# A hybrid decoder step: TensorE's issue order in the mixing stage, array shapes of its sample steps, and the bank of a transposed page

## The chip, the cores and the metric

The kernel runs on one core of one Trainium2 chip. The metric is the time of one execution on the device, in microseconds (us); the figure for a kernel is the median of several executions. Before the change it is 1176.64 us, the median of 3 runs (1175.74 to 1176.77).

In the profile PE is the matrix engine (TensorE), PEld its weight loads, DVE is VectorE, ACT is ScalarE, POOL is GpSimd, SP issues most DMAs.

## The reference

One layer for 512 new prompt tokens and 8 x 4 sample tokens: a half-step SwiGLU FFN, a token mixer, a second half-step FFN. The change lies in the mixer.

```python
def token_mix(h, past_k, past_v, C0, n0, m0, rel_bias, lam_init,
              w_in, b_gates, lam_q, lam_k, attn_norm, mlstm_norm, w_out):
    proj = h @ w_in
    ...
    q_a, k_a, v_a, q_m, k_m, v_m, o_m, gates = jnp.split(proj, idx, axis=-1)
    ...
        attn = diff_attention(q_a, k_all, v_all, q_pos, k_pos, rel_bias, lam)
    attn = (rmsnorm(attn, attn_norm) * (1.0 - lam_init)).reshape(B, S, H_ATT * ATT_DV)
    ...
    h_m, C, n, m = mlstm_chunkwise(...)
    h_m = rmsnorm(h_m, mlstm_norm).astype(h.dtype).reshape(B, S, H_ML * ML_DH) * jax.nn.sigmoid(o_m)
    mixed = jnp.concatenate([attn.astype(h.dtype), h_m], axis=-1)
    return mixed @ w_out, k_rows, v_a, C, n, m

def diff_attention(q, k, v, q_pos, k_pos, rel_bias, lam):
    logits = jnp.einsum('bqhcd,bkhcd->bchqk', q, k, preferred_element_type=jnp.float32) * (ATT_DQ ** -0.5)
    ...
    p = jax.nn.softmax(logits, axis=-1)
    a = p[:, 0] - lam * p[:, 1]
    return jnp.einsum('bhqk,bkhd->bqhd', a.astype(v.dtype), v)
```

There are 4 attention heads and 4 mLSTM heads of width 128. A sample's past keys and values, 512 rows, lie in pages of 128 rows that a page table picks from a cache.

## The kernel before

Activations are held with features on partitions and the 544 tokens (512 prompt, 32 sample) as columns, in two halves of 288 and 256 tokens. Every weight product is computed to about fp32 precision from two parts of each operand: L222, L223 and L224 multiply high by high, high by low and low by high. One output tile of 128 features and one half of the tokens takes 8 contraction tiles x 3 = 24 matmuls, into one bank of the pool `acc` (three banks). A weight tile is loaded as `raw` (SP), its high part `wh` is cast on ACT (L208), its low part `wl` subtracted on DVE (L209).

The mixing stage is a row of such products (q, k, v of each attention head; q, k, v of each mLSTM head; the output gates; then w_out), and between them run the heads' own steps. Those are written as Python generators in five queues of `side` (`prep`, `attn`, `ml`, `mls`, `smp`); `run` (L1350) advances every queue by one step after each product half. A step ends at a `yield`.

- `attn_head` (L896) starts one `attn_block` per 128 queries, up to three at a time. A block's scores are L958 (four matmuls; 128, 256, 384 or 512 keys wide). Their operands are split as well: `key_parts` (tile `cs`, L930 on ACT and L931 on DVE) once a head, and `query_parts` (tile `vb`, L940 on ACT and L942 on DVE) once a block; `vb` has one buffer, so a block's queries are split after the block before has used its own. The softmax follows on DVE (L966) and ACT (L969), then transposes L984, the value product L990, a norm, and the transpose L892 in `head_out`.
- `attn_samples` (L1000) gathers key pages from the cache (L1007, POOL, tile `pgin`, seven buffers), transposes each with four fp32 matmuls (L1033), copies it out on ACT (L1034, tile `pgT`), and multiplies it with the sample queries: the scores L1021 (page pairs) and L1060 (new keys), then transposes L1079 and L1084 of the probabilities, and the value products L1092 and L1096. L1021, L1060, L1092 and L1096 address 32 columns of the array at a time, four heads or samples beside one another; everything else uses 128. The mLSTM's L1254 is of the 32-column kind too.
- `ml_head` (L1133) runs an mLSTM head in four chunks: per chunk the state update L1170, the numerator L1178 and L1180, `ml_norm` (L1121; ACT and DVE), and L892 of the chunk before. `ml_sample_head` (L1211) updates the sample states.
- `out_gate` (L1298) is the gate product; behind each of its halves the queue `ml` is advanced twice.

PSUM has the pools `acc` (3 banks), `aux` (3, head steps) and `smp` (2, sample steps).

What sets the order: the instructions of each engine stand in a list that the scheduler of the language builds. By default it does not keep the program's order but places instructions by its own estimate of when they are ready, so that a step's matmuls may stand in the middle of a product, or another step's matmuls in the middle of a step. A context `tc.manual_schedule(engines=...)` keeps the named engines in the program's order; before the change only the kernel's setup uses it.

Of the kernel before, what the change touches and what calls it, by code (L numbers as in the profile page):

```python
# [10 lines left out]
F32 = mybir.dt.float32  # L11
# [165 lines left out]
class _Builder:  # L177
# [718 lines left out]
    def attn_head(self, h, k, v, side):  # L896
        nc = self.nc
        hd = self.hd
        kt = hd.tile([128, 4, 128], F32, name="kt")
        vt = hd.tile([128, 4, 132], F32, name="vt")  # L900
        for qb in range(4):
            side.add("attn", self.attn_block(h, qb, self.X[:, 4 + h, :], k, vt))
            if qb < 2:
                yield
        self.tok_major(v, vt[:, :, 0:128])
        nc.gpsimd.dma_start(out=self.o["v_prompt"][0, 0].rearrange("(b p) h d -> p b h d", p=128)[:, :, h, :],
                            in_=vt[:, :, 0:128])
        yield
        self.tok_major(k, kt)
        nc.gpsimd.dma_start(out=self.o["k_prompt"][0, 0].rearrange("(b p) h d -> p b h d", p=128)[:, :, h, :], in_=kt)  # L910
        nc.vector.tensor_copy(out=self.kas[:, h, :], in_=k[:, SEQ:T])
        nc.vector.tensor_copy(out=self.vas[:, h, :], in_=v[:, SEQ:T])
        self.new_keys += 1
# [31 lines left out]
    def attn_block(self, h, qb, q, k, vt):  # L945
        nc = self.nc
        wk = self.wk
        n = (qb + 1) * 128
        if qb == 0:
            self.key_parts(k)  # L950
            self.query_parts(q[:, 0:n])
            yield
        P = []
        z = wk.tile([128, 6], F32, name="z", bufs=6)
        for c in range(2):
            ps = self.ps_tile()
            for a in range(2):
                nc.tensor.matmul(ps[:, 0:n], lhsT=self.qt[:, 2 * a + c, :], rhs=self.ks[c][:, 0:n],  # L958
                                 start=a == 0, stop=a == 1)
            L = wk.tile([128, 512], F32, name="L", bufs=5)  # L960
            f = max(n - 256, 0)
            strip = self.strip[:, h, :]
            if f:
                nc.vector.tensor_tensor_reduce(L[:, 0:f], ps[:, 0:f], strip[:, 0:1].to_broadcast([128, f]), 1.0, -3.0e38,
                                               ALU.add, ALU.max, z[:, 4 + c:5 + c])
            nc.vector.tensor_tensor_reduce(L[:, f:n], ps[:, f:n], strip[:, 256 - n + f:256], 1.0,  # L966
                                           z[:, 4 + c:5 + c] if f else -3.0e38, ALU.add, ALU.max, z[:, c:c + 1])
            nc.vector.tensor_scalar_mul(z[:, c:c + 1], z[:, c:c + 1], -1.0)
            nc.scalar.activation(out=L[:, 0:n], in_=L[:, 0:n], func=AF.Exp, bias=z[:, c:c + 1],  # L969
                                 accum_out=z[:, 2 + c:3 + c])  # L970
            P.append(L)
        self.blocks_left -= 1
        if qb < 3:
            self.query_parts(q[:, n:n + 128])
        nc.vector.reciprocal(out=z[:, 2:4], in_=z[:, 2:4])
        nc.vector.tensor_tensor(out=z[:, 3:4], in0=z[:, 3:4], in1=self.nlam, op=ALU.mult)
        nc.vector.tensor_scalar(out=P[1][:, 0:n], in0=P[1][:, 0:n], scalar1=z[:, 3:4], scalar2=None, op0=ALU.mult)
        nc.vector.scalar_tensor_tensor(out=P[0][:, 0:n], in0=P[0][:, 0:n], scalar=z[:, 2:3], in1=P[1][:, 0:n],
                                       op0=ALU.mult, op1=ALU.add)
        yield  # L980
        yield
        ps = self.ps_tile()
        for kb in range(qb + 1):
            nc.tensor.transpose(ps[:, kb * 128:kb * 128 + 128], P[0][:, kb * 128:kb * 128 + 128], self.ident)  # L984
        aT = wk.tile([128, 512], F32, name="aT", bufs=2)
        nc.scalar.copy(out=aT[:, 0:n], in_=ps[:, 0:n])
        yield
        po = self.ps_tile()
        for kb in range(qb + 1):
            nc.tensor.matmul(po[:, 0:128], lhsT=aT[:, kb * 128:kb * 128 + 128], rhs=vt[:, kb, 0:128],  # L990
                             start=kb == 0, stop=kb == qb)
        y = wk.tile([128, 128], F32, name="y", bufs=3)
        nc.scalar.activation(out=y, in_=po[:, 0:128], func=AF.Square, accum_out=z[:, 4:5])
        self.rstd_act(z[:, 4:5], DH, z[:, 4:5])
        nc.vector.tensor_scalar(out=y, in0=po[:, 0:128], scalar1=z[:, 4:5], scalar2=None, op0=ALU.mult)
        yield
        self.head_out(y, self.X[:, h, qb * 128:qb * 128 + 128], 0)


    def attn_samples(self):  # L1000
# [4 lines left out]
        def page(which, b, pg):  # L1005
            t = self.pg.tile([128, 512], F32, name="pgin", bufs=7)
            nc.gpsimd.indirect_dma_start(out=t[:, 0:512], out_offset=None, in_=caches[which],  # L1007
                                         in_offset=IndirectOffsetOnAxis(ap=self.idx[:, b * NPG + pg:b * NPG + pg + 1], axis=0))
            return t[:, 0:512]
# [5 lines left out]
        for g in range(2):  # L1015
            lg = self.smp.tile([128, 512], F32, name="smp")
            todo_scores = []

            def scores(p, j, kT):
                for h in range(H):  # L1020
                    nc.tensor.matmul(lg[32 * h:32 * h + 32, p * 256:p * 256 + 256], lhsT=self.qz[:, 4 * g + j, h, :],  # L1021
                                     rhs=kT[:, h, :], start=j == 0, stop=j == 3, tile_position=(0, 32 * h))
            for p in range(NPG // 2):
                for j in range(4):
                    kT = self.pg.tile([128, H, 256], F32, name="pgT", bufs=3)
                    for e in range(2):
                        kp = ahead.pop(0)
                        i = todo.index((g, 2 * p + e, j)) + AHEAD
                        if i < len(todo):
                            ahead.append(page(0, 4 * todo[i][0] + todo[i][2], todo[i][1]))  # L1030
                        ps = self.smp.tile([128, 512], F32, name="smp")
                        for h in range(H):
                            nc.tensor.transpose(ps[:, h * 128:h * 128 + 128], kp[:, h * 128:h * 128 + 128], self.ident)  # L1033
                        nc.scalar.copy(out=kT[:, :, e * 128:e * 128 + 128], in_=ps.rearrange("p (h k) -> p h k", h=H))  # L1034
                    if len(todo_scores) == 2:
                        while todo_scores:
                            scores(*todo_scores.pop(0))
                    todo_scores.append((p, j, kT))
                    if p == 1 and j == 1:
                        vps = [page(1, 4 * g + jj, 0) for jj in range(4)]  # L1040
                    yield
            if g == 0:
                while self.new_keys < H:
                    yield
                for src, dst, name in ((self.vas, vtok, "v_sample"), (self.kas, None, "k_sample")):
                    ps = self.smp.tile([128, 512], F32, name="smp")
# [30 lines left out]
            ps = self.smp.tile([128, 512], F32, name="smp")  # L1077
# [35 lines left out]
            ps = self.smp.tile([128, 512], F32, name="smp")  # L1113
# [206 lines left out]
    def mix(self, hs, ws, gpost, finish, before):  # L1320
        nc, tc = self.nc, self.tc
# [15 lines left out]
        with ExitStack() as ctx:  # L1337
# [10 lines left out]
            def tile_of(name):  # L1348
                return self.hd.tile([128, T], F32, name=name)
# [10 lines left out]
            with gkp as gk:  # L1360
# [4 lines left out]
                k, v = tile_of("k"), tile_of("v")  # L1365
# [10 lines left out]
                for half in range(2):  # L1376
                    ps = [self.acc_tile(half)]
# [42 lines left out]

            self.new_keys = 0
            self.blocks_left = 4 * H
            side.add("prep", self.attn_head(0, k, v, side))
            run(project(*((aq[h], asc) for h in range(1 + NQ, H))))
            for h in range(H):
# [6 lines left out]
            for h in range(1, H):  # L1432
                k, v = tile_of("k"), tile_of("v")
# [35 lines left out]
            def mixed(half):  # L1469
                a, b = self.h_tiles(half)  # L1470
                for k in range(KT):
                    y = self.X[:, k, self.cols(half)]
                    nc.scalar.copy(out=a[:, k, :], in_=y)
                    nc.vector.tensor_tensor(out=b[:, k, :], in0=y, in1=a[:, k, :].bitcast(F32), op=ALU.subtract)
                ms.append((a, b, None))
# [9 lines left out]
            def mat(i, m, w, half):  # L1485
                if i == 3:
                    nc.scalar.dma_start(out=self.X[:, :, self.cols(half)], in_=xd[:, :, self.cols(half)])
                ps = self.acc_tile(half)
                _run(self.mmh(ps, w, ms, half))
                self.post_evac(ps, m, half, gpost, i == 0)  # L1490
            mixed(0)
            for i in range(KT):
                mat(i, *ws[max(0, i + KEPT - KT)], 0)
# [148 lines left out]
```

## Time and profile before

| | |
|---|---|
| median of 3 runs | 1176.64 us (1175.74 to 1176.77) |
| the profiled execution | 1174.52 us |
| its span in the profile | 1172.7 us |
| its mean granted TensorE clock | 0.997 |
| products of the mixing section, 456.66 to 735.87: L222, L223, L224 | 126.3, 123.9 and 123.1 us busy |
| L1033, page transposes | 19.5 us busy |
| L958, attention scores | 17.5 us busy, 3.8 us idle before them |
| L1096 and L1021, sample values and scores | 13.3 and 11.0 us busy |

The span is the time from the first to the last recorded instruction; the execution's own time is 1.8 us more. Busy times of matmuls overlap, since a matmul is recorded until it has left the array while the next is already streaming; what one costs is read from the distance of starts. A row of a timeline gives the start, the time, the engine, the line, the operation, output and inputs with their shapes (`128*32` is an operand of 32 array columns), and how many matmuls are joined in the row; in brackets stands how long the engine was idle before it and what ended that.

### The profile page before, as it was taken

Reading aid. Unit: us, or ns where it says so; the run is one execution under the profiler, and the core shown is the slowest. Engines: PE = TensorE matmul, PEld = TensorE weight load, DVE = VectorE, ACT = ScalarE, POOL = GpSimd, SP = SyncE. Lnnn points to the kernel's source line nnn. Section 1 sums busy time; section 2 is a strip of 40 time slices with the busy share of each in tenths; the row PEclk is TensorE's granted clock in tenths of the full one; section 3 lists DMA queues with packets and bytes.
Section 4 is the critical chain, followed back from the end, with each engine's and each line's share of the span. In section 5 each row is a group of like instructions: output and inputs, shape, how many; then the busy total and the mean of one; then the engine's idle time right before and its main releaser. Section 6 shows DMA issues by size and latency. Waiting matters only on the chain.

```text
span 1172.7 us, 22926 instructions
## 1 busy us (share of the span) xinstructions
PE 1154.3 (98%) x9182; PEld 1116.9 (95%) x9182; DVE 654.4 (56%) x1633; ACT 524.6 (45%) x1259; POOL 113.4 (10%) x155
## 2 busy tenths in 40 slices
PE   8999999999999999999999999999999999999997
PEld 7999999999999998899789879999999999999997
DVE  6755454554223698668675567885545454522334
ACT  6533332333323565767554456763333333332333
POOL 0000000000000043421234441000000000000000
PEclk9999999999999999999999999999999999999999
DMA  7322322222333464543355554532322322133334
GB/s 190 127 73 74 106 89 93 73 93 80 99 91 108 134 178 143 172 136 86 91 162 166 181 158 159 170 103 78 108 73 73 108 85 97 50 99 99 100 99 126
DMA packets 157545, 132.89 MB, mean 113 GB/s; under 512 B 5437, under 2 KB 149157, under 8 KB 157440
## 3 DMA queue, kind: packets, MB, share of 16 engines
q1 hardware_dynamic: 146576, 102.00, 29.2%
q0 software_dynamic: 8624, 27.05, 7.3%
q10 hardware_dynamic: 2240, 2.38, 0.6%
q8 instruction: 72, 1.18, 0.4%
q14 instruction: 33, 0.27, 0.1%
HBM read 122.35 MB, written 9.59 MB: 113 GB/s over the span
## 4 chain that ended last, share of the span: by engine, by line
PE 92%; DVE 3%; DMA 2%; ACT 1%; issue 1%; POOL 0%; DVEq 0%; POOLq 0%; ACTq 0%
PE acc L222 27%; PE acc L223 27%; PE acc L224 26%; PE smp L1096 1%; PE smp L1033 1%; PE aux L958 1%; PE aux L990 1%; DMA pgin<-in_cache_k_dram,idx 1%; PE aux L576 1%; DMA raw<-in_ffn_w_down_dram 1%; PE smp L222 1%; PE smp L224 1%; PE smp L223 1%; DVE vb L942 0%; PE smp L1021 0%
## 5 line engine op out<-in xcount | busy, mean ns | idle before, releaser
L222 PE MATMUL acc<-h,wh 128*128 128x256 f32 (+1 forms) x1896 | 552.8, 292 | 0.0
L223 PE MATMUL acc<-h,wh 128*128 128x256 f32 (+1 forms) x1896 | 547.7, 289 | 0.0
L224 PE MATMUL acc<-h,wl 128*128 128x256 f32 (+1 forms) x1896 | 545.1, 288 | 0.0
L209 DVE TENSOR_TENSOR wl<-raw,wh 128x512 fp32r<-128x512 f32 x378 | 251.1, 674 | 205.4 <-ACT wh L208 202.3
L222 PEld LDWEIGHTS acc<-h,wh 128*128 128x128 f32 x1896 | 357.0, 188 | 8.1 <-issue 7.5
L224 PEld LDWEIGHTS acc<-h,wl 128*128 128x128 f32 x1896 | 358.2, 189 | 0.6 <-issue 0.6
L223 PEld LDWEIGHTS acc<-h,wh 128*128 128x128 f32 x1896 | 357.5, 189 | 0.9 <-issue 0.4
L208 ACT CAST wh<-raw 128x512 fp32r<-128x512 f32 x378 | 225.6, 607 | 251.8 <-PE acc L223 198.4
L223 PE MATMUL acc<-ul,wh 128*128 128x288 f32 (+1 forms) x704 | 202.6, 288 | 0.0
L222 PE MATMUL acc<-uh,wh 128*128 128x288 f32 (+1 forms) x704 | 202.3, 287 | 0.0
L224 PE MATMUL acc<-uh,wl 128*128 128x288 f32 (+1 forms) x704 | 201.8, 287 | 0.0
L222 PEld LDWEIGHTS acc<-uh,wh 128*128 128x128 f32 x704 | 132.2, 188 | 0.1
L223 PEld LDWEIGHTS acc<-ul,wh 128*128 128x128 f32 x704 | 132.2, 188 | 0.1
L224 PEld LDWEIGHTS acc<-uh,wl 128*128 128x128 f32 x704 | 132.2, 188 | 0.1
L411 ACT CAST uh<-uu 128x288 fp32r<-128x288 f32 x88 | 36.9, 420 | 149.2 <-DVE uu L410 149.1
L409 DVE TENSOR_TENSOR uu<-acc,r 128x288 f32<-128x288 f32 (+1 forms) x84 | 37.0, 440 | 113.2 <-PE acc L224 107.9
L402 ACT ACTIVATE sg<-sg 128x288 f32<-128x288 f32 (+1 forms) x84 | 36.0, 430 | 93.7 <-DVE sg L394 93.5
L394 DVE TENSOR_TENSOR sg<-acc,r 128x288 f32<-128x288 f32 x84 | 37.0, 441 | 56.9 <-PE acc L224 52.4
L412 DVE TENSOR_TENSOR ul<-uu,uh 128x288 fp32r<-128x288 f32 x88 | 38.6, 439 | 22.0 <-ACT uh L411 22.0
L410 DVE TENSOR_TENSOR uu<-uu,sg 128x288 f32<-128x288 f32 x88 | 38.8, 441 | 6.6 <-ACT sg L402 1.1
L1329 POOL DMA_DIRECT2D x_keep<-X x2 | 1.8, 896 | 360.8 <-DVE X L325 360.8
L1007 POOL DMA_INDIRECT pgin<-in_cache_v_dram,idx x32 | 33.2, 1036 | 34.8 <-PE smp L1033 15.2
(386 smaller groups left out, 1081.3 us busy)
## 6 DMA issues: line engine op xcount, KB each, us to landing
raw<-in_ffn_w_gate_dram SPq DMA_DIRECT2D x20, 1024.0 KB, 5.1
raw<-in_ffn_w_up_dram SPq DMA_DIRECT2D x20, 1024.0 KB, 5.2
raw<-in_ffn_w_down_dram SPq DMA_DIRECT2D x20, 1024.0 KB, 6.3
raw<-in_w_in_dram SPq DMA_DIRECT2D x28, 512.0 KB, 4.3
raw<-in_ffn_w_down_dram SPq DMA_DIRECT2D x20, 384.0 KB, 3.7
raw<-in_w_out_dram SPq DMA_DIRECT2D x7, 1024.0 KB, 5.8
raw<-in_ffn_w_gate_dram SPq DMA_DIRECT2D x4, 512.0 KB, 6.2
raw<-in_ffn_w_up_dram SPq DMA_DIRECT2D x4, 512.0 KB, 6.4
```

Of the source, the lines that this page charges most:

```text
L208: nc.scalar.copy(out=wh[:, 0:n], in_=s)
L209: nc.vector.tensor_tensor(out=wl[:, 0:n], in0=s, in1=wh[:, 0:n].bitcast(F32), op=ALU.subtract)
L222: nc.tensor.matmul(ps, lhsT=wh, rhs=xh(k0 + k), start=st, stop=False)
L223: nc.tensor.matmul(ps, lhsT=wh, rhs=xl(k0 + k), start=False, stop=False)
L224: self.last_mm = nc.tensor.matmul(ps, lhsT=wl, rhs=xh(k0 + k), start=False, stop=sp).ins
L394: nc.vector.tensor_tensor(out=sg, in0=pg, in1=self.rs(hs, half), op=ALU.mult)
L402: nc.scalar.activation(out=sg, in_=sg, func=AF.Silu)
L409: nc.vector.tensor_tensor(out=uu, in0=pu, in1=self.rs(hs, half), op=ALU.mult)
L410: nc.vector.tensor_tensor(out=uu, in0=uu, in1=sg, op=ALU.mult)
L411: nc.scalar.copy(out=uh[:, m, sl], in_=uu)
L412: nc.vector.tensor_tensor(out=ul[m][:, sl], in0=uu, in1=uh[:, m, sl].bitcast(F32), op=ALU.subtract)
L1007: nc.gpsimd.indirect_dma_start(out=t[:, 0:512], out_offset=None, in_=caches[which], in_offset=IndirectOffsetOnAxis(ap=self.idx[:, b * NPG ...
```

## The change

Four things are changed, all in the mixing stage.

1. From just before the first `attn_head` until just before `mixed(0)`, that is, over all heads, sample steps and output gates, TensorE keeps the program's order. The other engines are scheduled as before.
2. Head 0's key and first query parts are emitted one step earlier, in `attn_head`, with a `yield` behind them; its first block then skips them.
3. In a sample step the pending scores are emitted ahead of the page transposes instead of behind them.
4. The second page of each pair is transposed into a bank of `acc` instead of `smp`.

```diff
@@ attn_head
+        if h == 0:
+            self.key_parts(k)
+            self.query_parts(self.X[:, 4, 0:128])
+            yield
         for qb in range(4):
             side.add("attn", self.attn_block(h, qb, self.X[:, 4 + h, :], k, vt))
@@ attn_block
         if qb == 0:
-            self.key_parts(k)
-            self.query_parts(q[:, 0:n])
+            if h:
+                self.key_parts(k)
+                self.query_parts(q[:, 0:n])
             yield
@@ attn_samples
                 for j in range(4):
+                    if len(todo_scores) == 2:
+                        while todo_scores:
+                            scores(*todo_scores.pop(0))
                     kT = self.pg.tile([128, H, 256], F32, name="pgT", bufs=3)
                     for e in range(2):
...
-                        ps = self.smp.tile([128, 512], F32, name="smp")
+                        ps = self.acc.tile([128, 512], F32, name="acc") if e else self.smp.tile([128, 512], F32, name="smp")
...
-                    if len(todo_scores) == 2:
-                        while todo_scores:
-                            scores(*todo_scores.pop(0))
                     todo_scores.append((p, j, kT))
@@ mix
             self.blocks_left = 4 * H
+            order = tc.manual_schedule(engines={mybir.EngineType.PE})
+            order.__enter__()
             side.add("prep", self.attn_head(0, k, v, side))
...
+            order.__exit__(None, None, None)
             mixed(0)
```

No instruction is added or removed; the lines below the edits move by 4 to 5 (L958 is L963 after, L1033 is L1041, L1096 is L1101, L1170, L1178 and L1180 are L1175, L1183 and L1185). TensorE's order at three places:

Head 0's first two score groups. TensorE before, from the last product of the half ahead (`h` is the high or low part of the activations, `vb` the split queries, `cs` the split keys):

```order
L224 MATMUL acc<-h_4823,wl 128x256
L958 MATMUL aux<-cs,vb 128x128 x4
L222 MATMUL acc<-h_4516,wh 128x288
L223 MATMUL acc<-h_4517,wh 128x288
L224 MATMUL acc<-h_4516,wl 128x288
L222 MATMUL acc<-h_4516,wh 128x288
L223 MATMUL acc<-h_4517,wh 128x288
L958 MATMUL aux<-cs,vb 128x256
L224 MATMUL acc<-h_4516,wl 128x288
```

TensorE after, from the end of the following half, whose 24 products now stand ahead:

```order
L224 MATMUL acc<-h_4516,wl 128x288
L963 MATMUL aux<-cs,vb 128x128 x4
L963 MATMUL aux<-cs,vb 128x256 x4
L1041 MATMUL smp<-base,pgin 128x128 x4
L1041 MATMUL acc<-base,pgin 128x128 x4
L222 MATMUL acc<-h_4823,wh 128x256
```

The two groups, which had products between them and between the second's four matmuls, now stand side by side, one product half later, with a page pair's transposes behind them.

A value step of the first sample group. TensorE before, while head 3's third score group and the first mLSTM head's state update are due (`saT` holds the transposed probabilities, `kt` the weighted keys):

```order
L224 MATMUL acc<-h_4823,wl 128x256
L958 MATMUL aux<-cs,vb 128x384 x4
L1096 MATMUL smp<-pgin,saT 32x512
L1170 MATMUL aux<-vt,kt 128x130
L1096 MATMUL smp<-pgin,saT 32x512 x3
L222 MATMUL acc<-h_4516,wh 128x288
```

TensorE after, at the gap that holds the same state update and the next value step:

```order
L224 MATMUL acc<-h_4823,wl 128x256
L892 MATMUL aux<-base,y 128x128
L963 MATMUL aux<-cs,vb 128x128 x4
L963 MATMUL aux<-cs,vb 128x256 x4
L1175 MATMUL aux<-vt,kt 128x130
L1183 MATMUL aux<-vt,L 128x130
L1101 MATMUL smp<-pgin,saT 32x512 x4
L222 MATMUL acc<-h_4516,wh 128x288
```

The value step's matmuls stand together; before, the state update stood behind the first of the four.

A gap behind an output gate's half. TensorE before (`y` holds the normed rows, `C` the state, `L` and `vt` weights and values of a chunk):

```order
L1178 MATMUL aux<-vt,L 128x130
L1180 MATMUL aux<-C,L 128x130
L892 MATMUL aux<-base,y 128x128
L1021 MATMUL smp<-pgT,qz 32x256 x3
L1224 MATMUL aux<-base,sm 128x128 x2
L1225 MATMUL aux<-sm 128x32
L1021 MATMUL smp<-pgT,qz 32x256 x5
L1060 MATMUL smp<-kas,qz 32x32 x16
L1170 MATMUL aux<-vt,kt 128x130
L222 MATMUL acc<-h_4516,wh 128x288
L223 MATMUL acc<-h_4517,wh 128x288
L224 MATMUL acc<-h_4516,wl 128x288
```

TensorE after, the same gap:

```order
L1183 MATMUL aux<-vt,L 128x130
L1185 MATMUL aux<-C,L 128x130
L892 MATMUL aux<-base,y 128x128
L1026 MATMUL smp<-pgT,qz 32x256 x8
L1065 MATMUL smp<-kas,qz 32x32 x16
L1175 MATMUL aux<-vt,kt 128x130
L1183 MATMUL aux<-vt,L 128x130
L1185 MATMUL aux<-C,L 128x130
L892 MATMUL aux<-base,y 128x128
L222 MATMUL acc<-h_4516,wh 128x288
L223 MATMUL acc<-h_4517,wh 128x288
L224 MATMUL acc<-h_4516,wl 128x288
```

The scores L1021 stand together, and the second chunk's numerator and the transpose L892 of the chunk before it, which stood behind three products, now stand ahead of the products.

## The prediction

> **What bounds the kernel now.** I read the page first, then busy time by stretch, then the list of waits, then the timeline of TensorE and its neighbours where those waits stand. The page:
>
> ```profile
> span 1172.7 us, 22926 instructions
> PE 1154.3 (98%) x9182; PEld 1116.9 (95%) x9182; DVE 654.4 (56%) x1633; ACT 524.6 (45%) x1259; POOL 113.4 (10%) x155
> PE 92%; DVE 3%; DMA 2%; ACT 1%; issue 1%; POOL 0%; DVEq 0%; POOLq 0%; ACTq 0%
> ```
>
> TensorE is busy for 98% of the span and makes up 92% of the chain that ended last. Neither its instructions nor their sizes change, so there are only two things to win or lose: time in which it stands still, and time in which it works worse than the same matmuls can (half clock, or broken array shapes). The change touches the mixing section, from head 0's scores at 456.66 to the last head's state update at 735.87:
>
> ```profile
> 456.66:735.87 279.21, 272.45 (x2212) 242.41 (x2211) 193.41 (x692) 169.93 (x509) 92.01 (x111) 0.99 0.49 150
> 463.00:467.00 4.00, 4.00 (x20) 4.00 (x21) 3.69 (x18) 2.55 (x10) 2.28 (x4) 0.60 0.88 243
> ```
>
> The columns are the stretch, its length, the busy time of PE, PEld, DVE, ACT and POOL, the granted clock, DMA share and GB/s. TensorE idles 279.21 - 272.45 = 6.8 us here. One stretch of 4 us has a granted clock of 0.60: 4.00 x (1 - 0.60) = 1.6 us more are lost in it. So **8.4 us** at most can be won from waits. VectorE (193 of 279) and ScalarE (170) are not the bound, but both stand between one step of a head and its next. The waits:
>
> ```profile
> PE aux L958 <- ACT vb L940: 1.7, 2, 1.5
> PE aux L958 <- DVE vb L942: 1.6, 3, 0.8
> PE smp L1033 <- DMA pgin<-in_cache_k_dram,idx: 1.3, 1, 1.3
> PE aux L1140 <- DVE X L893: 0.4, 1, 0.4
> ```
>
> The columns are the sum, the count and the longest. About half belongs to the attention scores L958, which need the split queries of L940 and L942. It is one place:
>
> ```profile
> 459.37 0.27 PE L224 MATMUL acc<-h,wl 128*128 128x256 f32 x1
> 461.17 0.32 PE L958 MATMUL aux<-cs,vb 128*128 128x128 f32 x1 [1.52 <-ACT vb L940]
> 462.31 0.44 PE L958 MATMUL aux<-cs,vb 128*128 128x128 f32 x2 [0.83 <-DVE vb L942]
> 462.94 0.48 PE L958 MATMUL aux<-cs,vb 128*128 128x128 f32 x1 [0.18 <-DVE vb L942]
> 463.21 0.55 PE L222 MATMUL acc<-h,wh 128*128 128x288 f32 x1
> ...
> 466.69 0.29 PE L222 MATMUL acc<-h,wh 128*128 128x288 f32 x1
> 466.82 0.29 PE L223 MATMUL acc<-h,wh 128*128 128x288 f32 x1
> ```
>
> The idle times in brackets are 2.5 us together. The half clock comes right behind: products start .13 us apart again only from 466.69 on (466.82 - 466.69).
>
> **The change part by part.** *One array shape per step.* TensorE's L1021, L1060, L1092, L1096 and L1254 use 32 of its columns, all else 128. Counted in the two orders, this section has 28 runs of the narrow shape before and 18 after; eight of the ten that go are halves of a step that something cut. What a cut costs:
>
> ```profile
> 569.58 1.04 PE L1096 MATMUL smp<-pgin,saT 128*32 128x512 f32 x8
> 570.55 0.40 PE L222 MATMUL acc<-h,wh 128*128 128x288 f32 x1
> 570.79 0.29 PE L223 MATMUL acc<-h,wh 128*128 128x288 f32 x1
> ...
> 580.44 1.05 PE L1096 MATMUL smp<-pgin,saT 128*32 128x512 f32 x2
> 581.42 0.49 PE L1170 MATMUL aux<-vt,kt 128*128 128x130 f32 x2
> 581.84 1.06 PE L1096 MATMUL smp<-pgin,saT 128*32 128x512 f32 x6
> 582.83 0.40 PE L222 MATMUL acc<-h,wh 128*128 128x288 f32 x1
> ```
>
> Whole, the eight passes take 570.55 - 569.58 = .97 us. Cut, they take .98 (to 581.42) and .99 (581.84 to 582.83): a cut costs 1.00 us, and four of L1096's eight groups are cut: 4.0 us. [...]
>
> ```profile
> 503.28 1.05 PE L1021 MATMUL smp<-pgT,qz 128*32 128x256 f32 x10
> 504.26 0.66 PE L1033 MATMUL smp<-base,pgin 128*128 128x128 f32 x4
> 504.85 0.63 PE L1021 MATMUL smp<-pgT,qz 128*32 128x256 f32 x6
> 505.41 0.39 PE L222 MATMUL acc<-h,wh 128*128 128x256 f32 x1
> ...
> 634.29 1.07 PE L1021 MATMUL smp<-pgT,qz 128*32 128x256 f32 x16
> 635.29 0.40 PE L224 MATMUL acc<-h,wl 128*128 128x288 f32 x1
> ```
>
> The score group L1021 takes 1.00 whole and .98 + .56 cut, so .54 more; four of its eight are cut: 2.2 us. Two more narrow runs join a neighbour (half a us each by the .54: 1.0). Returns from the fp32 and narrow steps to the products fall by 19 in the two orders; the first product behind one takes .24 us (570.55 to 570.79) instead of .13, so 19 x .10 = 1.9. Sum: 4.0 + 2.2 + 1.0 + 1.9 = **9.1 us gained**. Bounds: 6.2 (the cuts alone) and 9.1. These matmuls run on the busy engine, so nothing hides the gain.
>
> *Program order on TensorE.* Before, products of the neighbouring half ran in the middle of a chain of dependent steps; now they can't. All 8.4 us of old waits I count as gone, and set the new ones beside them.
>
> First pair. After, head 0's L958 of 128 and of 256 columns stand side by side, behind a whole half of 24 products. These start where the old stall did (459.37 + .27 = 459.64) and need weights whose second part VectorE splits here:
>
> ```profile
> 461.68 1.21 DVE L942 TENSOR_TENSOR vb<-X,vb 64x128 fp32r<-64x128 f32 x4
> 462.91 0.69 DVE L209 TENSOR_TENSOR wl<-raw,wh 128x512 fp32r<-128x512 f32 x1
> ```
>
> Twelve of the 24 products take 1.6 us (.13 each) and end at 461.2; the next wait for the split's end, 462.91 + .69 = 463.60: 2.4 us. Then the 256-column scores wait for queries that can only be split when the 128-column ones have left the one buffer:
>
> ```profile
> 495.92 0.56 PE L958 MATMUL aux<-cs,vb 128*128 128x128 f32 x4
> 496.31 0.62 PE L1033 MATMUL smp<-base,pgin 128*128 128x128 f32 x4
> ...
> 497.24 0.39 PE L958 MATMUL aux<-cs,vb 128*128 128x256 f32 x1 [0.17 <-ACT vb L940]
> 497.46 0.29 PE L223 MATMUL acc<-h,wh 128*128 128x288 f32 x1
> ...
> 499.08 0.39 PE L958 MATMUL aux<-cs,vb 128*128 128x256 f32 x1
> ```
>
> That chain is 499.08 - 496.31 = 2.8 us from the end of the first group to the start of the second's last matmul. Before, products and transposes ran in it (the row at 497.46 is one). After, nothing does, as the pages' L1033 stand behind the scores. First pair: 2.4 + 2.8 = **5.2 us lost**; 4.0 if head 0's parts, emitted a step earlier, put the 1.2 us of L942 out of the way of the weight split. I keep 5.2, since the cast of the same weights on ScalarE has those parts ahead of it too. The earlier parts take away the 1.5 us wait on L940, not the second chain. Two more pairs, heads 1 and 3, stand the same way, with their weights there: 2.8 each, less three of the four score matmuls that run within it at .2 each (497.24 to 497.46), 2.2: **4.4 us** (bounds for both: 1.6, half the chain less those matmuls, and 5.6, the whole of it). Head 2's groups stay apart.
>
> Chains of the mLSTM heads:
>
> ```profile
> 676.63 0.39 PE L1180 MATMUL aux<-C,L 128*128 128x130 f32 x2
> ...
> 678.60 1.16 PE L1079 MATMUL smp<-s,Ls 128*128 128x128 f32 x8
> 679.59 0.39 PE L1084 MATMUL smp<-s,Ls 128*128 128x128 f32 x2
> 679.82 0.27 PE L892 MATMUL aux<-base,y 128*128 128x128 f32 x1
> ```
>
> From a chunk's numerator L1180 to the transpose L892 of its normed rows lie 3.2 us, through ScalarE and VectorE. In the last stretch four gaps between products hold two mLSTM steps each after the change, and their second L892 has only some 2.1 us of work ahead of it (a sample step of 1.00, as L1079 and L1021, and the next step's short matmuls): 3.2 - 2.1 = 1.1 short, **4.2 us** for the four. About ten other gaps hold a step whose input was made one product half earlier (24 x .12 = 2.9 to 24 x .13 = 3.1 us against 3.2): .1 each, **1.0 us**; bounds 0 and .4, the wait of L1140 on a normed row in the list above. If the cover of one product half is gone there, each costs .4 or more.
>
> *Scores ahead of the transposes, second page in an acc bank.* L1033 then waits for its page and a free bank. The one old wait of 1.3 on a page is within the 8.4; the loads' issue on POOL moves four loads ahead of state loads. I take nothing, from -.4 to +.5, a third of that wait either way. A price would come where the products want that acc bank before the copy out of it is done; the products ask for one bank per 24 matmuls, about 3 us.
>
> **Sum:** -9.1 - 8.4 + 5.2 + 4.4 + 4.2 + 1.0 = **-2.7 us**, against the profiled execution's 1174.5 us (span 1172.7): 1171.8. The median of the runs shown, 1176.64, stands 2.1 above that, so **1173.9**.
>
> **Rivals.** *The order gives nothing but the shapes.* The ten other gaps wait .3 each, near the .4 of that row: 2.0 more, 1175.9, no difference that a measurement of this kernel can tell (0.2% is 2.35 us). For it: 8.4 us of old waits against 14.8 new ones.
>
> *The clock halves again.* In this trace 2.5 us of idleness within 3.8 us came ahead of the clock of 0.60; the 1.3 us wait for a page did not (the section's mean clock of .99 leaves room for the one stretch: 1.6 of 279). The first pair's two waits (2.4 and 2.8, with 1.6 of products between) are of that size, so its 1.6 us would come back: 1173.9 + 1.6 = 1175.5, again no difference. [...]
>
> *Chains in a row (slower).* With TensorE strictly in order, a late input holds everything behind it. VectorE's and ScalarE's queues also carry the weight splits (69% and 61% of the section busy), so that each of the fourteen gaps may be short by .85 rather than by .37 on average: 14 x .85 = 11.9 instead of 5.2, +6.7: 1180.6. It decides from 14 gaps x .73 on: there the sum is above +2.35. For it: 3.2 against 2.9 leaves no reserve. Against it: before, TensorE waited for such chains only .4 at a time, though in an order that filled them.
>
> *The change does not do what it says.* If narrow runs cost nothing in the new surroundings (9.1 not won), the same waits give +6.4: 1183.0. Cuts of .98 and .99 speak against it.
>
> **How the numbers follow.** As summed: .45, 1173.9 (faster by 0.23%; its own range is 1166 to 1174.3). Only the shapes: .16. Clock: .11. Chains: .25. No shapes: .03. Faster .45, same .16 + .11 = .27, slower .25 + .03 = .28. The best end takes 4.0 for the first pair, 1.6 for the others, and a third of the gaps, 1.7: -17.5 + 7.3 = -10.2, 1166.4. The worst end short of the last rival: shapes 6.2 and waits 6.8 won, 5.2 + 5.6 + 4.2 + 4.0 lost: +6.0, 1182.6. I leave a little out on either side: 1166 to 1182.
>
> **What would show it.** Cuts: no narrow group of fewer than 16 (scores) or 8 (L1096) passes in the timeline, and the section's fp32 and narrow lines costing less. Pairs: three waits of 2 to 3 us of the 256-column scores on the query split, the first behind a half with a hole of about 2.4. Gaps: waits of about 1 us of L892 on the normed rows. A second stretch with a clock near .6 shows the clock rival; an idle total above 20 us in the section the chain rival. The prediction is wrong if the idle time of the section stays under 8, or if products themselves run slower than .13.

## The result and the profile after

The changed kernel takes 1188.9 us (median of 4 runs, 1186.6 to 1195.3) beside 1176.3 of the kernel before on the same chip: a ratio of **1.0124** (95% interval 1.0108 to 1.0140), 1.2% slower. Forecast were 1173.9 us and a range of 1166 to 1182. The profiled execution took 1186.6 us, the least of the four; its span is 1184.8. Of the executions reported further down one stands apart, 1739.1 us at a granted clock of .60 with the order up to the mLSTM heads; the ratio there leaves it out. The page of the changed kernel:

```profile
span 1184.8 us, 22921 instructions
PE 1151.8 (97%) x9182; PEld 1118.1 (94%) x9182; DVE 658.1 (56%) x1633; ACT 523.4 (44%) x1259; POOL 112.1 (9%) x155
PE 87%; DVE 6%; ACT 3%; issue 2%; DMA 2%; POOL 0%; DVEq 0%; POOLq 0%; ACTq 0%; SPq 0%
```

TensorE is busy a little less (1151.8 us instead of 1154.3), and its share of the chain that ended last falls from 92% to 87%; VectorE's doubles. The stretch from the product half ahead of head 0's scores to the same statistics matmul (L254) at the end of the first w_out half, in the kernel before and then in the changed kernel, with two shorter stretches of the latter (stretch, length, busy PE, PEld, DVE, ACT, POOL, clock, DMA share, GB/s):

```profile
456.66:763.22 306.56, 299.80 (x2438) 269.66 (x2436) 217.89 (x742) 192.93 (x565) 92.55 (x112) 0.99 0.50 151
```

```profile
456.36:775.40 319.04, 297.61 (x2437) 271.10 (x2436) 221.45 (x739) 191.80 (x564) 91.29 (x112) 0.98 0.49 144
460.00:520.00 60.00, 54.33 (x434) 50.65 (x432) 37.68 (x135) 38.33 (x110) 24.64 (x28) 0.94 0.57 167
580.00:640.00 60.00, 55.07 (x411) 47.57 (x411) 43.34 (x160) 30.74 (x106) 16.97 (x20) 0.97 0.44 124
```

The whole difference lies here: 319.04 - 306.56 = 12.5 us. TensorE idles 319.04 - 297.61 = **21.4 us** instead of 6.8. The clock takes 60 x .06 + 60 x .03 = **5.4 us**, where the one slow stretch of before took 1.6. Idleness and clock are 14.6 + 3.8 = 18.4 us more, so by what is left over the work itself became 18.4 - 12.5 = **5.9 us** shorter. The waits of the changed kernel in this stretch (sum, count, longest):

```profile
PE aux L963 <- ACT vb L944: 4.3, 4, 2.6
PE aux L892 <- DVE y L1135: 3.7, 4, 1.8
PE aux L963 <- DVE vb L946: 3.0, 5, 1.6
PE aux L885 <- ACT aT L991: 2.1, 2, 1.5
PE acc L1041 <- DMA pgin<-in_cache_k_dram,idx: 1.7, 1, 1.7
PE aux L1175 <- ACT aT L991: 1.2, 2, 0.7
PE aux L892 <- DVE C L1180: 0.8, 1, 0.8
PE acc L222 <- issue: 0.8, 1, 0.8
PE aux L885 <- DVE z L971: 0.7, 1, 0.7
PE aux L963 <- DVE z L971: 0.7, 1, 0.7
PE aux L1183 <- DVE z L971: 0.4, 1, 0.4
```

Before, the list ended after a handful of entries; now nearly every kind of head step waits somewhere. L963 (scores) waits 7.3 us on the query splits: 3.2, 2.4 and .8 in the pairs of heads 0, 1 and 3, the rest ahead of head 2's first scores. L892 waits 4.5: 3.7 on normed rows, all of it in the last stretch, that of the output gates (four places from 678.7 to 716.7), and .8 on a state. The remaining 21.4 - 11.8 = 9.6 us have several causes. The largest is a bank of the pool `aux`: L885, L1175, L963 and L1183 wait 2.1 + 1.2 + .7 + .7 + .4 = 5.1 us for L991 and L971. They read nothing that these write, but L991 and L971 empty a bank of `aux` that an attention block has filled. The longest of them, TensorE and then ScalarE:

```profile
561.60 0.60 PE L995 MATMUL aux<-vt,aT 128*128 128x128 f32 x4
562.04 0.49 PE L989 MATMUL aux<-base,L 128*128 128x128 f32 x3
562.29 0.48 PE L1145 MATMUL aux<-rw,sel 128*128 128x512 f32 x1
564.25 0.66 PE L885 MATMUL aux<-base,k 128*128 128x128 f32 x4 [1.49 <-ACT aT L991]
```

```profile
563.74 0.46 ACT L991 COPY aT<-aux 128x384 f32<-128x384 f32 x1
```

L995, L989 and L1145 fill the three banks, and the transposes L885 of an mLSTM head start when the first of them is free: the copy L991 of the attention block's transposes L989 ends at 563.74 + .46 = 564.20. Besides these waits there are a page (1.7), .8 without a named cause at a place where the edits without the order wait as long, and some 2.0 in small entries. Head 0's pair, on TensorE and then on ScalarE:

```profile
462.39 0.56 PE L963 MATMUL aux<-cs,vb 128*128 128x128 f32 x4
465.56 0.74 PE L963 MATMUL aux<-cs,vb 128*128 128x256 f32 x2 [2.61 <-ACT vb L944]
466.70 0.58 PE L963 MATMUL aux<-cs,vb 128*128 128x256 f32 x1 [0.40 <-ACT vb L944]
467.44 0.58 PE L963 MATMUL aux<-cs,vb 128*128 128x256 f32 x1 [0.16 <-DVE vb L946]
467.82 1.05 PE L1041 MATMUL smp<-base,pgin 128*128 128x128 f32 x4
```

```profile
463.04 0.30 ACT L944 CAST vb<-X 64x128 fp32r<-64x128 f32 x1 [0.75 <-PE aux L963]
464.70 0.40 ACT L974 ACTIVATE L<-L,z 128x128 f32<-128x128 f32 x1 [1.37 <-DVE z L973]
465.01 0.19 ACT L974 ACTIVATION_READ_ACCUMULATOR L<-L,z 128x1 f32 x1
465.21 0.30 ACT L944 CAST vb<-X 64x128 fp32r<-64x128 f32 x1
```

The 128-column scores no longer wait. The 256-column scores do: ScalarE makes the first of four query casts, then stands 1.37 us for a softmax step that is ahead of the next casts in its own order. From the start of the first group (462.39) to the page transposes (467.82) 5.4 us pass, of which 2.61 + .40 + .16 = 3.2 us are idle. Right behind, the granted clock falls to .65:

```profile
469.00:474.00 5.00, 5.00 (x31) 5.00 (x30) 3.15 (x11) 2.80 (x8) 3.00 (x5) 0.65 0.39 95
```

5 x .35 = 1.75 us are lost in this stretch alone. The other slow stretch, 585 to 590 with a clock of .66, stands behind head 3's pair.

### The profile page after: what moved, and what is told of

It is laid out like the page before. It is cut to its first block, busy times and chain, and to the rows that moved or that the text cites. A ratio compares the mean times of both kernels' runs of the same rounds, so it can differ in the third digit from the quotient of the medians.

```text
span 1184.8 us, 22921 instructions
## 1 busy us (share of the span) xinstructions
PE 1151.8 (97%) x9182; PEld 1118.1 (94%) x9182; DVE 658.1 (56%) x1633; ACT 523.4 (44%) x1259; POOL 112.1 (9%) x155
## 4 chain that ended last, share of the span: by engine, by line
PE 87%; DVE 6%; ACT 3%; issue 2%; DMA 2%; POOL 0%; DVEq 0%; POOLq 0%; ACTq 0%; SPq 0%
PE acc L222 26%; PE acc L223 26%; PE acc L224 26%; DVE wl L209 1%; DVE vb L946 1%; PE aux L576 1%; PE aux L995 1%; DMA pgin<-in_cache_k_dram,idx 1%; PE smp L1101 1%; PE aux L963 1%; PE smp L222 1%; PE smp L223 1%; PE smp L224 1%; PE smp L1041 0%; PE acc L1041 0%
## 5 line engine op out<-in xcount | busy, mean ns | idle before, releaser
L1012 POOL DMA_INDIRECT pgin<-in_cache_k_dram,idx x32 | 32.6, 1019 | 39.2 <-PE smp L1041 25.2
```

## The experiments

Each ratio below is to the kernel before on the same chip, with its 95% interval. Theory A: program order exposes chains of dependent steps; A1 has most of it in the pairs of attention scores and the low clock behind them (.65 and .66 above), A2 in the many gaps. Theory B: the other edits cost the time.

**The order alone, and the other edits alone.** The first takes only the two lines of `manual_schedule` into the kernel before, the second takes only these lines out of the changed one.

```diff
+            order = tc.manual_schedule(engines={mybir.EngineType.PE})
+            order.__enter__()
             side.add("prep", self.attn_head(0, k, v, side))
...
+            order.__exit__(None, None, None)
             mixed(0)
```

> Program order on TensorE alone; head 0's parts, the place of the scores and the bank as before the change. Theory A (the order itself exposes chains of dependent steps, and the three other edits win some of it back): slower than the changed kernel or like it, 1188 to 1195 us. Theory B (the other edits cost the time, above all pages transposed in an acc bank that the products want): near or below the kernel before, 1172 to 1178.

> The three other edits with the scheduler's own order on TensorE. Theory A: within 4 us of the kernel before, 1172 to 1179. Theory B: most of the 12.6 us is still lost, 1183 or more.

Measured: the order alone 1200.2 us, ratio 1.0218 (1.0192 to 1.0245); the edits alone 1178.4, 1.0025 (1.0014 to 1.0036). B is out as the main cause: without the order the other edits cost .25%, 2.8 us. It is the order that costs, and the edits together win back half of its cost. In the order's own profile one wait stands out:

```profile
PE smp L1033 <- ACT pgT L1034: 11.7, 10, 2.5
```

**The bank.** The changed kernel with the second page in `smp` again.

```diff
-                        ps = self.acc.tile([128, 512], F32, name="acc") if e else self.smp.tile([128, 512], F32, name="smp")
+                        ps = self.smp.tile([128, 512], F32, name="smp")
```

> The changed kernel with the second page transposed in an smp bank again. If the pages' copies on ScalarE hold TensorE in program order (11.7 us of waits of the transposes on the copy with the order alone), a good part of them comes back: 1191 to 1197. If the acc bank costs the products more than it saves: 1184 to 1188.

Measured 1205.3 us, 1.0257 (1.0234 to 1.0280), and the wait is back:

```profile
PE smp L1041 <- ACT pgT L1042: 12.1, 11, 2.7
```

In program order the third bank is worth some 16 us: with two `smp` banks a transpose must wait for ScalarE's copy of an earlier page, and everything on TensorE behind it waits too. It is more than was expected, and more than the order costs in the end. The profiles agree: over 400 to 820 TensorE idles 33.6 us instead of 21.4, and the clock takes 9.0 instead of 5.4. Beside the order alone (1.0218) this kernel, which has the early parts and the scores ahead as well, is no faster, so what wins back half of the order's cost is the bank. The scores ahead were not run by themselves.

**The early parts of head 0**, taken out of the changed kernel (edit 2 undone).

```diff
-        if h == 0:
-            self.key_parts(k)
-            self.query_parts(self.X[:, 4, 0:128])
-            yield
...
-            if h:
-                self.key_parts(k)
-                self.query_parts(q[:, 0:n])
+            self.key_parts(k)
+            self.query_parts(q[:, 0:n])
```

> The changed kernel without the early parts of head 0. In program order nothing covers the first split: the old stall of 2.5 us and its half clock come back beside the pair's chain, 2 to 5 us slower than the changed kernel: 1191 to 1194. If the pair's chain swallows it: 1188 to 1190.

Measured 1189.3, 1.0136 (1.0118 to 1.0154): not told apart from the changed kernel. The old stall is back, but the second group then waits less: all waits of head 0's two groups are 3.3 us together, beside 3.2 in the changed kernel. The pair's chain swallows the old stall.

**Where the order costs.** Program order up to the first mLSTM head's products, and from there on.

```diff
-            order.__exit__(None, None, None)
             mixed(0)
...
+            order.__exit__(None, None, None)
             for h in range(H):
                 qkv = [tile_of(n) for n in "qkv"]
```

> The changed kernel with TensorE in program order only until the products of the first mLSTM head begin (the attention heads' part); the scheduler orders the rest. With the edits alone the kernel takes 1178.4, with the order over all of it 1188.9: 10.5 us to be divided. Theory A1 (pairs of attention scores and the half clock behind them): most of it is here, 1185 to 1188. Theory A2 (gaps of the mLSTM heads): 1179 to 1183.

> The other part alone: TensorE in program order from the first mLSTM head's products on, the scheduler's order ahead of it. Theory A1: 1179 to 1182 (pair 3 of head 3 still falls in this part). Theory A2: 1184 to 1188. If the two parts add up, this and the run before are together about 10.5 us above twice the 1178.4 of the edits alone.

Measured 1182.9, 1.0067 (1.0046 to 1.0087), and 1185.8, 1.0092 (1.0075 to 1.0108). Over the 1178.4 of the edits alone that is 4.6 and 7.5 us, together 12.1, near the 10.5 of the whole. Both parts cost, the second more: neither A1 nor A2 alone. The second part still holds head 3's pair. In the profiles, over 400 to 820, TensorE idles 11.6 us with the first part in order and 19.3 with the second, so most of the new idleness lies in the second; the clock takes 3.6 us in the first and nothing in the second.

**The pairs apart.** One more step behind a head's first block.

```diff
             if qb < 2:
                 yield
+            if qb == 0:
+                yield
```

> The changed kernel with one more yield behind a head's first block, so that the 128-column and the 256-column scores of heads 0, 1 and 3 stand one product half apart. Theory A1 (the three pairs, with the half clock that they bring, are the larger part of the loss: 8 to 12 us): 1177 to 1181. Theory A2 (the many small gaps are the larger part, the pairs some 4 us): 1183 to 1187. In both the waits of L963 on the query split (7.3 us in the changed kernel's profile) fall below 2.

Measured 1191.0, 1.0129 (1.0106 to 1.0152): no gain, outside the ranges of both theories, though the waits of the scores on the splits fell from 7.3 to 2.4 us and the mean clock of the span is .997 as in the kernel before. The extra step pushed the end of the heads back, and a value step there met a page that was not yet loaded (TensorE of this kernel, lines two higher):

```profile
719.43 1.05 PE L1103 MATMUL smp<-pgin,saT 128*32 128x512 f32 x2
723.10 3.99 PE L1103 MATMUL smp<-pgin,saT 128*32 128x512 f32 x6 [2.63 <-DMA pgin<-in_cache_v_dram,idx]
727.02 0.61 PE L222 MATMUL acc<-h,wh 128*128 128x288 f32 x1
```

The group takes 727.02 - 719.43 = 7.6 us instead of 1.0: it waits 2.6 for the load, and its last six passes take 3.9. The run doesn't decide between A1 and A2; here the step that was moved lost elsewhere what it won.

**Two buffers for the split queries** (and two for transposed pages, to make room).

```diff
-        self.qt = qt = self.pg.tile([128, 4, 128], F32R, name="vb", bufs=1)
+        self.qt = qt = self.pg.tile([128, 4, 128], F32R, name="vb", bufs=2)
```

> The changed kernel with two buffers for the split queries instead of one (and two instead of three for transposed pages, to make room), so that a block's queries can be split before the block before has used its own. Theory A1 (the one buffer makes the pairs' chain): the waits of L963 on the split (7.3 us) fall under 3, the stretch at half clock behind head 0's pair goes, and the time falls by 8 to 11 us to 1178 to 1181. Theory A2: it falls by 3 to 5, 1184 to 1186. If the scheduler splits the second block's queries late for its own reasons, or the page copies wait for a buffer, nothing is won: 1188 to 1190.

Measured 1183.1, 1.0064 (1.0043 to 1.0085): 5.8 us less than the changed kernel. The wait on the split is gone, and another stands in its place:

```profile
464.22 1.53 PE L963 MATMUL aux<-cs,vb 128*128 128x128 f32 x6
469.03 0.77 PE L963 MATMUL aux<-cs,vb 128*128 128x256 f32 x2 [3.28 <-DVE z L971]
```

```profile
466.41 1.90 DVE L209 TENSOR_TENSOR wl<-raw,wh 128x512 fp32r<-128x512 f32 x3
468.23 0.45 DVE L871 TENSOR_TENSOR k<-acc,r 128x288 f32<-128x288 f32 x1
468.59 0.28 DVE L971 CUSTOM_DVE_ANT_0 L<-aux,strip 128x128 f32<-128x128 f32 x1
```

Two of the four 256-column matmuls now run at once (x6 is four of the first group and two of the second); the other two need an `aux` bank, which VectorE empties (L971) only after three weight splits and a product's evacuation, 2.3 us. So the one buffer was a part of the pair's chain, not all of it; VectorE's queue is the next. About half of what is won is the clock: over 400 to 820 TensorE idles 18.0 us instead of 21.4, and the clock takes 1.8 us instead of 5.4. The 1.8 stand behind head 0's pair still.

**The sample step first in each gap**, so that the head steps have its work ahead of them.

```diff
+        side.queue("smp", 1)
         side.queue("prep", 1)
...
-        side.queue("smp", 1)
```

> The changed kernel with the sample step's queue advanced first in every gap, ahead of the heads' steps, so that each head step has 1 to 2 us of page transposes and scores ahead of it. Theory A2 (small gaps): the waits of L892, L885 and L1175 on ScalarE and VectorE (8.5 us) fall by half, and the time to 1181 to 1185. Theory A1 (pairs): the pairs are as they were, since their chain starts after the sample step: 1186 to 1190.

Measured 1198.4, 1.0191 (1.0168 to 1.0213): 9.5 us slower than the changed kernel, against both theories:

```profile
PE aux L892 <- DVE y L1135: 7.0, 3, 2.9
```

Most of the loss is the clock. Over 400 to 820 it takes 14.4 us instead of 5.4, while TensorE idles 24.1 us instead of 21.4; the mean clock of the four executions is .987 to .990, in the changed kernel .991 to .995. Why L892 waits longer was not tried further. One reading is that the steps that start ScalarE's and VectorE's work now come later in each gap, so that less time is left before their results are needed.

**The norm two chunks back** in `ml_head` (with two buffers for transposed pages instead of three).

```diff
-            if last:
-                self.head_out(*last)
-            last = (y, self.X[:, 4 + h, s], 1)
+            if len(last) == 2:
+                self.head_out(*last.pop(0))
+            last.append((y, self.X[:, 4 + h, s], 1))
...
-        self.head_out(*last)
+        for args in last:
+            self.head_out(*args)
```

> The changed kernel with the transpose L892 of an mLSTM chunk two chunks behind its numerator instead of one (five buffers for the normed rows instead of three; two for transposed pages), so that its norm has a whole product half more. Theory A2 (gap chains): the waits of L892 on the normed rows (3.7 us in the profile, 6 with the idle sub-microseconds around them) fall under 1, the time falls by 3 to 6 us, 1183 to 1186. Theory A1: under 3 us, 1186 to 1189.

Measured 1189.7, 1.0141 (1.0110 to 1.0172): nothing won. The waits of L892 on normed rows are 4.1 us in three places instead of 3.7 in four, since a head's last chunk has no chunk behind it and still comes one step after its numerator. The largest of these waits, 2.0 us, is there. The changed kernel's last gap shows one of this kind:

```profile
712.71 0.39 PE L1185 MATMUL aux<-C,L 128*128 128x130 f32 x2
712.93 0.27 PE L892 MATMUL aux<-base,y 128*128 128x128 f32 x1
...
714.35 1.33 PE L1101 MATMUL smp<-pgin,saT 128*32 128x512 f32 x8
716.74 0.30 PE L892 MATMUL aux<-base,y 128*128 128x128 f32 x1 [1.06 <-DVE y L1135]
```

**The second mLSTM step in the middle of the gate's product**, alone and with the two query buffers.

```diff
-        _run(self.mmh(ps, w, hs, half))
+        gen = self.mmh(ps, w, hs, half)
+        for k, _ in enumerate(gen):
+            if k == 3:
+                between()
```

> The changed kernel with the second mLSTM step of an output gate's gap moved into the middle of the gate's product (behind 12 of its 24 matmuls). Theory A2 (two dependent steps too close in one gap): the waits of L892 on the normed rows (3.7 us) fall under 1.5 and the time by 2 to 5 us, to 1184 to 1187; eight more returns to the products cost 0.8 of it. If the chains are as late with products between: 1188 to 1190.

> e13 with the two query buffers of e7. If the two losses are separate, their gains add: 5.8 us of e7 and what e13 wins, 1178 to 1181. If the time is set by something else behind them: as e7, 1182 to 1184.

Measured 1190.4, 1.0141 (1.0118 to 1.0164), and 1179.2, 1.0047 (1.0030 to 1.0064). Alone it wins nothing: the longest wait of L892 falls from 1.8 to 1.0 us, but the four together stay at 3.6, and TensorE idles 21.7 us in all, as in the changed kernel. A reading is that the distance taken from one step is given to the next: two chunks of about 3.2 us of chain stand against one product half of about 3 us and the other steps' work. With two buffers it is 1179.2, within the range of gains that add; but the intervals don't tell 1.0047 from the 1.0064 of the buffers alone, and there was no gain of the first edit to add.

**Whole groups under the scheduler.** The kernel before, but each group of L1021 and L1096 is issued behind the last TensorE instruction traced ahead of it (`seen`, kept by a wrapper around matmul and transpose), which is the one that used to cut it.

```diff
+                with self.tc.issue_after(self.seen[0]):
+                    for h in range(H):
                         nc.tensor.matmul(lg[32 * h:32 * h + 32, p * 256:p * 256 + 256], lhsT=self.qz[:, 4 * g + j, h, :],
```

> The kernel before with the scheduler's order, but each group of score matmuls L1021 and of value matmuls L1096 issued behind the last TensorE instruction traced ahead of it, so that nothing stands inside a group: the eight cuts go, the order is otherwise the scheduler's. If a cut costs what the prediction took (1.00 and .54 us), 4.0 + 2.2 us are won, less short waits of the groups for the step now ahead of them: 1169.5 to 1173 beside 1175.7. If the gain of whole groups is only apparent (other work ran in the time of a cut): 1174 to 1177.

Measured 1173.5, .9980 (.9965 to .9996): faster, by little more than the interval and by less than the 6.2 us of the cuts. The cuts are all gone, and one group gave part of it back:

```profile
698.95 1.06 PE L1109 MATMUL smp<-pgin,saT 128*32 128x512 f32 x6
702.12 1.92 PE L1109 MATMUL smp<-pgin,saT 128*32 128x512 f32 x2 [2.12 <-DMA pgin<-in_cache_v_dram,idx]
703.97 0.58 PE L230 MATMUL acc<-h,wh 128*128 128x256 f32 x1
```

This group takes 703.97 - 698.95 = 5.0 us instead of 1.0, as the last page's load is late and the products that used to fill its place now stand behind it. 6.2 - 4.0 = 2.2 us fits what the times show (1175.7 to 1173.5), though the interval runs from .5 to 4.1 us.

**Two variants of it**: with the scores ahead of the transposes and two buffers each for queries and transposed pages, and with head 0's early parts (edit 2, as above).

> The kernel before with whole groups as in e9, the scores ahead of the transposes, two buffers for the split queries and two for transposed pages; the scheduler's order. The pairs' chain has products to fill it here, so the second buffer should be worth little over e9: the first stall (2.5 us and 1.6 of half clock) may shrink by 1 to 3 us if it hangs on the buffer, not if it hangs on the first split: 1168 to 1173.

> e9 with head 0's key and query parts one step earlier, as in the change. If the first stall of the kernel before (2.5 us on the parts and the half clock of 1.6 behind it) hangs on when the parts are emitted, 2 to 4 us less than e9; if the wait moves to the second block's queries, the same as e9 within 1.5 us.

Measured 1175.2, 1.0000 (.9988 to 1.0011), and **1172.4, .9971 (.9962 to .9981)**, which beats both kernels. The first is not faster than the whole groups alone, so its three edits together win nothing; what the second query buffer does by itself under the scheduler was not run. The early parts may be worth a little: the interval overlaps with that of the whole groups alone. The largest wait of the second kernel in this stretch is again on the second block's queries, 2.5 us instead of 2.8 on the first block's, so the stall moved and shrank little; what its profile no longer shows is the late page above:

```profile
PE aux L971 <- ACT vb L952: 2.5, 1, 2.5
```

## Why the prediction was wrong

The sum was -9.1 (shapes) - 8.4 (old waits) + 5.2 + 4.4 (pairs) + 4.2 (close mLSTM steps) + 1.0 (other gaps) = -2.7 us. By its own terms:

- **Other gaps, 1.0 us: the step that failed.** What is idle beyond the splits and L892 measured 9.6 us. The term priced one chain, from a numerator through the norm to L892, against one product half. That chain costs nothing in these gaps: L892 waits on normed rows only in the last stretch. What the term left out is the bank that each step needs. In program order a step of an mLSTM head stands behind one of an attention block in the same gap, and waits until ScalarE (L991) or VectorE (L971) has emptied one of the three `aux` banks: 5.1 us, of which .7 are of this kind within head 3's pair. A page (1.7), the .8 without a named cause and small entries are the rest. The slower rival ("with TensorE strictly in order, a late input holds everything behind it") was near in kind and in size: it took 11.9 us for fourteen gaps, .85 each, and L892's waits and the rest are 4.5 + 9.6 = 14.1. But much of it is a late bank and not a late input.
- **No term for the clock.** It was a rival of 1.6 us with a chance of .11. It is 5.4 us in the profile, 3.6 of it from 460 to 520 behind head 0's pair and 1.8 behind head 3's. The runs of the changed kernel show it too: 1186.6 us at a mean clock of .995, 1195.3 at .991; the .004 between them is about 4.8 of the 8.7 us. The mean clocks of the four executions go from .991 to .995, so the cost is not the same in each; behind which waits it fell was recorded in the profiled one alone.
- **Pairs, 9.6 us:** 6.3 on the splits, beside the .7 on a bank. The first pair was put at 2.4 + 2.8. The 2.4 did not come: the products ahead of it run without a wait up to 462.39. The chain behind the first group took longer instead: from the start of that group to the start of the second's last matmul pass 467.44 - 462.39 = 5.1 us, where the rows that the prediction went by have 499.08 - 495.92 = 3.2, because in ScalarE's order softmax steps stand between the casts. The other two pairs, put at 4.4, wait 3.2 and the .7. With two buffers the same place waits 3.28 us on VectorE.
- **Close mLSTM steps, 4.2 us:** L892 waits 3.7 us on normed rows, in the last stretch. Right in size and in place.
- **Shapes, 9.1 us:** the work became 5.9 us shorter. The traces show the 28 narrow runs before and 18 after that were counted, and a whole value group takes 1.00 us in the changed kernel, so the cuts are gone; that they are worth 6.2 fits the groups made whole under the scheduler. Of the two joins and the 19 returns (2.9 us) nothing is left to be seen.

```profile
599.98 1.06 PE L1101 MATMUL smp<-pgin,saT 128*32 128x512 f32 x8
600.98 0.40 PE L222 MATMUL acc<-h,wh 128*128 128x288 f32 x1
```

- **Scores ahead, second page in `acc`: nothing taken.** The bank is worth some 16 us in program order. The prediction did not see this, since it weighed all four edits at once; for the order without the bank its sum would have been too low by that much more.
- **Old waits, 8.4 us counted as gone:** the wait for head 0's first splits is gone. A page is still waited for (1.7 us instead of 1.3), and splits and norms are waited for at other places.

The terms that were off make up the whole miss: 8.6 (other gaps) + 5.4 (clock) + 3.2 (shapes) + .3 (L892) - 2.3 (splits) = 15.2 us, from the -2.7 that was forecast to the 12.5 that the profiles show.

What stays open: how much of the 7.5 us of the second part hangs on which chain. Both runs that stretched one chain there only moved the waits, which fits a limit set by all of them together, but no run took that limit away. That the 5.1 us are waits for a bank is read from the trace; no run changes the number of `aux` banks.

## What to carry to other kernels

Keeping an engine in program order trades fragments for waits: here the work became 5.9 us shorter, and the engine idled 14.6 us more. Price every chain that crosses the engine, and every buffer and bank that one step needs from another, against the cover that program order leaves it, and look for a low granted clock behind the new waits, which took 5.4 us here. Where only a few groups must stay whole, order those and leave the rest to the scheduler: here that is .2% faster, .3% with the early parts, where the full order is 1.2% slower. A buffer or bank that a scheduler makes unnecessary by filling its wait can become the largest term once the order is fixed: in the kernel before, with two `smp` banks, the page transposes wait .4 us for ScalarE's copies; with the order and the same two banks 12.1.

## What was not expected of the hardware

In some of these kernels a late page costs twice, in others not. Around the held group of the kernel with whole groups the granted clock is .66:

```profile
701.00:706.00 5.00, 3.88 (x13) 2.21 (x14) 1.54 (x5) 0.85 (x4) 1.47 (x3) 0.66 0.51 187
```

So 5 x .34 = 1.7 us are lost beside the 2.1 of the wait, although no other long wait stands near. A longer wait elsewhere does not: in the variant with two buffers each a value group waits 3.1 us for its page, and the clock is 1.00 around it:

```profile
706.36 1.04 PE L1109 MATMUL smp<-pgin,saT 128*32 128x512 f32 x2 [3.08 <-DMA pgin<-in_cache_v_dram,idx]
```

```profile
700.00:712.00 12.00, 8.92 (x61) 6.65 (x60) 6.53 (x23) 7.43 (x25) 2.34 (x5) 1.00 0.45 145
```

So in these profiles the length of a wait alone does not say whether the clock falls. In the kernel before it is 1.00 from 665 to 670, around a wait of 1.3 us for a page.
